# Turning the SSD rows on VectorE and through DRAM instead of on TensorE

## The chip, the cores and the metric

The kernel runs on one core of one Trainium2 chip. The metric is the device time of one launch in microseconds (us), as the median of several executions. The engines of a core each work through their own list of instructions in order and wait for each other by semaphores: TensorE (PE; its weight loads are listed as PEld), VectorE (DVE), ScalarE (ACT), GpSimd (POOL) and SyncE (SP), which here only issues transfers.

## The reference

One step of a hybrid decoder layer on T = 336 tokens (16 learned meta tokens, 256 prompt tokens, 8 sample sequences of 8 tokens), model width 2048, all in f32. Cut to its core:

```python
h = rms_norm(x, norm_w)
z, xbc, dt_raw, sc_b, sc_c, sc_h, sc_z, g_a, g_b = split_proj(h @ w_in)
# branch A: SSD. 64 heads of 64 in 8 groups, state 128, chunks of 128 tokens
xbc_c, conv_new = causal_dwconv(xbc, conv_prev, ssd_conv_w)        # width 4
xs, bm, cm = split(silu(xbc_c + ssd_conv_b))
dt = softplus(dt_raw + dt_bias); log_a = -dt * exp(a_log)
for each chunk:
    y      = (C.B^T * decay * dt) @ xs  +  exp(cumsum(log_a)) * C @ state
    state  = exp(sum(log_a)) * state + sum_j to_end_j * xs_j (x) B_j
y_a = gated_group_rms_norm(y + d_skip * xs, z, ssd_norm_w) @ w_ssd_out
# branch B: short gated conv
y_b = (sc_b * conv3(sc_c * sc_h) * silu(sc_z)) @ w_sconv_out
out = x + (sigmoid(g_a) * y_a + sigmoid(g_b) * y_b) @ w_o          # then a last rms_norm
```

Beside the two outputs, the new states of the two convolutions and of the SSD (for the prompt and for the samples) are returned.

## The kernel before

**Weights.** All weights come from HBM as blocks of 128 x 1024 f32. `wblk` (L90 to L97) takes a block through three tiles: `wraw` is loaded on SP's queue (L92), ScalarE rounds it to a high part `whi` (L94), VectorE subtracts to get the low part `wlo` (L96). Each of the three has three buffers (pool `wp`, `bufs=3`). `mm` (L109 to L115) spends a block as 24 matmuls: a first pass of 16 with `whi` (L111 against the high part of the activations, L112 against the low part) and a second pass of 8 with `wlo` (L115). There are 470 such splits in all. A projection (`proj`, `unit`) is two blocks into one PSUM tile `pj`, of which there are two.

**The group stage.** The eight groups of the SSD branch run in the pool `pb`. For a group g, `weave` traces these units of projection work one after the other: four `z_units` (two blocks each), eight `out_units` of group g-1 (one block each), for the first and last group four `gate_units`, and six `conv_units` of group g+1 (two blocks each: B, C, then the four tiles xs0 to xs3 of x). That is 28 blocks for a middle group. After each unit it advances the generator `ssd(g)`, which holds the scan of group g, by as many steps as are due (`NSTEP * past / total`), and `behind(tail)` ties each instruction of these steps behind the newest weight instruction of its engine (`latest`), so that steps stay at their place between the weight blocks. The scheduler then merges each engine's list; one list per engine is fixed when the kernel is built.

**The conv of a tile.** `conv_tile` copies the projection from PSUM to a padded tile (`pad`, two ScalarE copies, L462 and L463), applies the four taps into `cacc` (ScalarE L469, then three VectorE instructions L471) and the SiLU by a tanh (L474) and two VectorE instructions (L475, L476). The result has channels on the partitions and tokens in the free dimension.

**The scan needs rows.** The scan wants x and B with tokens on the partitions. `rows(c)`, one step for each of the chunk sets c = 0, 1, 2, does this on TensorE: four transposes of xs (L534), one of BT (L536), and beside them the product C.B (L537). VectorE multiplies by dt out of PSUM into `xdt` (L539), B is split into a high and a low part, and `cbm` takes the masked C.B. These visits, and the ones for the chunk state (L585, `state`), for y (L650) and for the samples' state (L713), stand between two weight blocks on TensorE. Later steps of the same generator are the sum over the group norm (`pr`, L701 to L705), the update of the samples' state (`up`, two halves, each two additions `h` on VectorE, L716), and the scaled y with its split (`ys` L726, `yh` L727, `yl` L728), from which group g's `out_units` in the next weave are fed.

## Time and profile before

| | |
|---|---|
| median of three runs | 1822.84 us (1822.80 to 1824.69) |
| the profiled execution | 1824.75 us, its span 1823.0 us |
| granted TensorE clock | 1.0 |
| TensorE busy | 1814.9 us, 100% of the span |
| VectorE busy | 1147.7 us, 63% |
| ScalarE busy | 828.8 us, 45% |
| GpSimd busy | 389.4 us, 21% |
| moved by DMA | 331 MB, 182 GB/s on average |
| length of a middle group's weave | 111.4 us |

In the profile, "L96 DVE TENSOR_TENSOR wlo<-wraw,whi" is an instruction of line 96 on VectorE that writes `wlo`. In a timeline the first number is the start in us from the start of the span and the second the duration; a bracket gives the idle time just before and what ended it. Matmuls overlap, so what a matmul costs TensorE is the distance from one start to the next and not the duration printed.

### The profile page before, as it was taken

How to read it: one execution, taken by the hardware profiler on the slowest of the kernel's cores; microseconds unless marked ns; L12 is line 12 of the kernel's file. 1: busy time of each engine (PE TensorE's matmuls, PEld its weight loads, DVE VectorE, ACT ScalarE, POOL GpSimd, SP SyncE). 2: the span in 40 equal slices, each digit the busy share in tenths (PEclk: the TensorE clock that was granted, in tenths of full speed). 3: DMA queues.
4: the chain of work that ended last, by engine and by line, in shares of the span. 5: the costliest groups of instructions: out<-in, count | busy, mean ns of one | idle time of the engine just before them, and what ended most of it. 6: DMA issues, size and time to landing. Idle time of an engine off the chain costs nothing.

```text
span 1823.0 us, 32410 instructions
## 1 busy us (share of the span) xinstructions
PE 1814.9 (100%) x13006; PEld 1798.0 (99%) x13006; DVE 1147.7 (63%) x1696; ACT 828.8 (45%) x1269; POOL 389.4 (21%) x398
## 2 busy tenths in 40 slices
PE   9999999999999999999999999999999999999998
PEld 9999999999999999999999999999999999999998
DVE  7745544444543335668587787877778777776544
ACT  6433333333333334645656354564546545343543
POOL 0000000000000001253162433524334252400012
PEclk9999999999999999999999999999999999999999
DMA  7444444444444446457566574665656657476553
GB/s 254 146 151 150 150 149 149 145 152 151 156 152 159 160 162 227 149 178 240 163 201 223 177 246 150 208 215 178 238 157 211 206 169 249 153 243 213 184 175 129
DMA packets 117286, 331.33 MB, mean 182 GB/s; under 512 B 20944, under 2 KB 37904, under 8 KB 117136
## 3 DMA queue, kind: packets, MB, share of 16 engines
q1 hardware_dynamic: 116272, 327.89, 55.9%
q8 instruction: 102, 1.67, 0.4%
q10 hardware_dynamic: 864, 1.38, 0.2%
q14 instruction: 48, 0.39, 0.1%
HBM read 296.34 MB, written 32.88 MB: 181 GB/s over the span
## 4 chain that ended last, share of the span: by engine, by line
PE 96%; DMA 2%; ACT 1%; DVE 1%; issue 0%; POOLq 0%; POOL 0%; SPq 0%; ACTq 0%; DVEq 0%
PE pj L111 30%; PE pj L112 30%; PE pj L115 29%; PE yb L650 2%; DMA wraw<-w 1%; PE ms L636 1%; PE pj L219 1%; PE yb L585 1%; PE pj L862 1%; ACT whi L94 0%; PE ms L534 0%; ACT W L559 0%; PE ms L219 0%; DMA ssms<-h 0%; PE yb L713 0%
## 5 line engine op out<-in xcount | busy, mean ns | idle before, releaser
L111 PE MATMUL pj<-hx,whi 128*128 128x320 f32 (+3 forms) x2880 | 864.4, 312 | 0.0
L112 PE MATMUL pj<-hx,whi 128*128 128x320 f32 (+3 forms) x2880 | 860.6, 311 | 0.0
L96 DVE TENSOR_TENSOR wlo<-wraw,whi 128x1024 fp32r<-128x1024 f32 x470 | 596.8, 1270 | 413.9 <-ACT whi L94 206.8
L94 ACT ACTIVATE whi<-wraw 128x1024 fp32r<-128x1024 f32 x470 | 496.7, 1057 | 768.0 <-PE pj L112 628.1
L111 PEld LDWEIGHTS pj<-hx,whi 128*128 128x128 f32 x2880 | 540.7, 188 | 4.6 <-ACT pad L462 1.7
L112 PEld LDWEIGHTS pj<-hx,whi 128*128 128x128 f32 x2880 | 541.5, 188 | 0.1
L115 PE MATMUL pj<-hx,wlo 128*128 128x320 f32 (+3 forms) x2880 | 485.4, 310 | 0.0
L115 PEld LDWEIGHTS pj<-hx,wlo 128*128 128x128 f32 x2880 | 440.6, 188 | 0.0
L111 PE MATMUL pj<-yh,whi 128*128 128x320 f32 x512 | 153.5, 311 | 1.2 <-ACT zs L503 0.9
L112 PE MATMUL pj<-yl,whi 128*128 128x320 f32 x512 | 152.3, 309 | 0.0
L596 POOL TENSOR_TENSOR h<-h,decS 128x512 f32<-128x512 f32 x64 | 76.4, 1227 | 147.5 <-PE ms L636 147.5
L111 PEld LDWEIGHTS pj<-yh,whi 128*128 128x128 f32 x512 | 96.2, 188 | 3.1 <-ACT zs L503 1.4
L112 PEld LDWEIGHTS pj<-yl,whi 128*128 128x128 f32 x512 | 96.3, 188 | 0.6
L115 PE MATMUL pj<-yh,wlo 128*128 128x320 f32 x512 | 95.8, 309 | 0.0
L242 POOL COPY SCS<-up 128x2 f32<-128x2 f32 x16 | 18.2, 1139 | 359.2 <-DVE up L236 329.0
L744 DVE TENSOR_TENSOR yan<-yan,pj 128x320 f32<-128x320 f32 x112 | 54.2, 485 | 62.9 <-PE pj L115 61.3
L471 DVE SCALAR_TENSOR_TENSOR cacc<-pad,V,cacc 128x360 f32<-128x360 f32 (+1 forms) x144 | 89.5, 621 | 2.0
L464 POOL COPY pad<-cs 128x24 f32<-128x24 f32 x48 | 56.2, 1172 | 126.6 <-DVE cacc L471 115.5
L115 PEld LDWEIGHTS pj<-yh,wlo 128*128 128x128 f32 x512 | 80.4, 188 | 0.0
L111 PE MATMUL pj<-vhi,whi 128*128 128x320 f32 x256 | 75.5, 308 | 0.0
L112 PE MATMUL pj<-vlo,whi 128*128 128x320 f32 x256 | 75.5, 308 | 0.0
L465 POOL COPY cs<-pad 128x3 f32<-128x3 f32 x48 | 45.0, 938 | 82.5 <-ACT pad L462 82.0
(286 smaller groups left out, 1721.7 us busy)
## 6 DMA issues: line engine op xcount, KB each, us to landing
wraw<-w SPq DMA_DIRECT2D x346, 512.0 KB, 3.9
wraw<-wso SPq DMA_DIRECT2D x64, 512.0 KB, 3.5
wraw<-wsc SPq DMA_DIRECT2D x32, 512.0 KB, 3.8
h<-h0T SPq DMA_DIRECT2D x32, 512.0 KB, 4.9
ssms<-h SPq DMA_DIRECT2D x32, 512.0 KB, 4.2
wraw<-wo SPq DMA_DIRECT2D x32, 512.0 KB, 3.9
xq_d<-xe SPq DMA_DIRECT2D x16, 320.0 KB, 3.4
W<-ac_d SPq DMA_DIRECT2D x8, 576.0 KB, 6.4
```

Source lines behind the costliest of these rows:

```text
L94: latest["act"] = nc.scalar.activation(hi[:, :n], raw[:, :n], AF.Copy).ins
L96: latest["dve"] = nc.vector.tensor_tensor(lo[:, :n], raw[:, :n], fb(hi[:, :n]), sub).ins
L111: nc.tensor.matmul(out, w, xh(k0 + k), start=first and k == 0, stop=False)
L112: nc.tensor.matmul(out, w, xl(k0 + k), start=False, stop=False)
L115: latest["pe"] = nc.tensor.matmul(out, w, xh(k0 + k), start=False, stop=last and k == nk - 1).ins
L219: nc.tensor.matmul(pu[i][:, :T - t0], w[:, o:o + P], x[:, k, t0:], start=k == 0 and j == 0, stop=k == 15 and j == 2)
L464: nc.gpsimd.tensor_copy(smp[:, :, 0:3], cs[:, 1:9, :])
L465: nc.gpsimd.tensor_copy(cs[:, 0, :], pad[:, 272:275])
L471: nc.vector.scalar_tensor_tensor(acc[:, i0:], pad[:, i0 + k:360 + k], col(V_CW, 4 * j + k), acc[:, i0:], mult, add)
L596: nc.gpsimd.tensor_tensor(split(h0[b]), split(h0[b]), bc(hv(decS[:, b, :], g), [P, 8, HP]), mult)
L650: nc.tensor.matmul(yb[q * HP:(q + 1) * HP, t, t0:t0 + n], x[:, h * HP:(h + 1) * HP], w[:, h, :], start=i == 0, stop=i == 3)
L744: nc.vector.tensor_tensor(ya[:, m, :TV], ya[:, m, :TV], pp[:, :TV], add)
```

## The change

`conv_tile` gets an argument `rows`: for B and the four tiles of x, VectorE transposes the finished tile in blocks of 32 x 32 (two instructions, 128x320 and 128x32, into the tile's own `cacc`), and four transfers of [32, 11, 32] put the blocks, now with tokens on the partitions, in their places in a DRAM tile `xr_d` of 352 x 640. These four are kept in a list and issued from ScalarE's queue by `flush()`, at the next `conv_tile` after its first tap, or in the first z unit of the next weave. `rows(c)` is gone. In its place `load(c)` reads the rows back on SP's queue, tied behind the newest weight load of SP (`latest["sp"]`, new), `cross()` computes the three C.B products in one visit, `rows_in(c)` multiplies by dt in SBUF and splits B, and `ends(c)` is the GpSimd part that stood in `weights(c)`. The steps are 25 instead of 23: `cross`, `decay(0)`, the exponential and the state loads, `decay(1)`, `weights(0)`, `weights(1)` with the loads, `rows_in(0)`, and so on. So the later steps (y, the norm's sum, the samples' state, the split of y) fall behind other units than before.

```diff
-NSTEP = 23
+NSTEP = 25
+XR = 352
...
+    xr_d = [dr.tile([XR, 640], F32, name=f"xr_d{i}") for i in range(2)]
...
     def wblk(src, n=1024):
         raw = wp.tile([P, 1024], F32, name="wraw")
-        nc.sync.dma_start(raw[:, :n], src)
+        latest["sp"] = nc.sync.dma_start(raw[:, :n], src).ins
         hi = wp.tile([P, 1024], F32R, name="whi")
         latest["act"] = nc.scalar.activation(hi[:, :n], raw[:, :n], AF.Copy).ins
         lo = wp.tile([P, 1024], F32R, name="wlo")
         latest["dve"] = nc.vector.tensor_tensor(lo[:, :n], raw[:, :n], fb(hi[:, :n]), sub).ins
         return hi, lo
+    def after(ins, a):
+        tc.add_manual_dep(ins, a.name, mybir.DependencyInfo(mybir.DependencyClass.NoSync,
+                                                            mybir.DependencyReason.DATA), reason="step")
     def behind(tail):
         for ins in reversed(nc.cur_bb.bb.instructions):
             if ins is tail:
                 break
-            for a in latest.values():
-                if ins.engine == a.engine:
-                    tc.add_manual_dep(ins, a.name, mybir.DependencyInfo(mybir.DependencyClass.NoSync,
-                                                                         mybir.DependencyReason.DATA), reason="step")
+            for k in ("act", "dve", "pe"):
+                if k in latest and ins.engine == latest[k].engine:
+                    after(ins, latest[k])
...
+        pend = []
+        def flush():
+            while pend:
+                nc.scalar.dma_start(*pend.pop(0))
+        def conv_tile(src, j, t0, out, cs, rows=None):
             pp = proj(src, t0)
...
             acc = pb.tile([P, 360], F32, name="cacc")
             nc.scalar.activation(acc[:, i0:], pad[:, i0:360], AF.Identity, bias=col(V_CB, j), scale=col(V_CW, 4 * j))
+            flush()
             for k in range(1, 4):
                 nc.vector.scalar_tensor_tensor(acc[:, i0:], pad[:, i0 + k:360 + k], col(V_CW, 4 * j + k),
...
                 acc[:, 272:360].rearrange("p (b t) -> p b t", t=11)[:, :, 3:11], add, mult)
+            if rows is not None:
+                nc.vector.transpose(acc[:, :320], out[:, :320])
+                nc.vector.transpose(acc[:, 320:XR], out[:, T - 32:])
+                to, c = rows
+                for a in range(0, P, 32):
+                    pend.append((to.rearrange("(b q) c -> q b c", q=32)[:, :, c + a:c + a + 32],
+                                 acc[a:a + 32, :XR].rearrange("p (b f) -> p b f", f=32)))
         def conv_units(g, st):
...
+            to = xr_d[g % 2]
             BT = st["BT"] = pb.tile([P, T], F32, name="BT")
-            conv_tile(w1[64 + g], 32 + g, 0, BT, cs[:, 4])
+            conv_tile(w1[64 + g], 32 + g, 0, BT, cs[:, 4], (to, 512))
             yield
...
             for t in range(4):
-                conv_tile(w1[32 + 4 * g + t], 4 * g + t, 0, xs[:, t, :], cs[:, t])
+                conv_tile(w1[32 + 4 * g + t], 4 * g + t, 0, xs[:, t, :], cs[:, t], (to, P * t))
...
                 nc.scalar.activation(th, pz, AF.Tanh, scale=0.5)
                 nc.scalar.activation(z[:, :TV], pz, AF.Copy)
+                flush()
...
+            bt = [pb.tile([P, 2, P], F32R, name="bh0", bufs=1), free[:, 1024:1280].rearrange("p (i n) -> p i n", n=P),
+                  pb.tile([P, P], F32, name="bt", bufs=1)]
+            def load(c):
+                xdt[c] = big("xdt", 3)
+                b = bt[c] if c == 2 else fb(bt[c][:, 1, :])
+                rows = xr_d[g % 2]
+                for o, r, n in ((0, P * c, P),) if c < 2 else ((0, 256, 64), (64, 336, 16)):
+                    for d, q in ((xdt[c], slice(0, 512)), (b, slice(512, 640))):
+                        after(nc.sync.dma_start(d[o:o + n], rows[r:r + n, q]).ins, latest["sp"])
+            def cross():
                 pq = ps.tile([P, 512], F32, name="ms")
-                nc.tensor.transpose(pq[:n, 0:P], BT[:, t0:t0 + n], ident)
-                nc.tensor.matmul(pq[:n, P:P + m], BT[:, t0:t0 + n], CT[:, TGT[c]:TGT[c] + m], start=True, stop=True)
-                xdt[c] = big("xdt", 3)
-                nc.vector.tensor_tensor(split(xdt[c][:n]), split(pp[:n]), bc(hv(dtt[:n, c, :], g), [n, 8, HP]), mult)
-                if c == 2:
-                    bt[c] = pb.tile([P, P], F32, name="bt", bufs=1)
-                    nc.scalar.activation(bt[c][:n], pq[:n, 0:P], AF.Copy)
-                else:
-                    bt[c] = (free[:, 1024:1280].rearrange("p (i n) -> p i n", n=P) if c else
-                             pb.tile([P, 2, P], F32R, name="bh0", bufs=1))
-                    nc.scalar.activation(bt[c][:, 0, :], pq[:, 0:P], AF.Copy)
-                    nc.vector.tensor_tensor(bt[c][:, 1, :], pq[:, 0:P], fb(bt[c][:, 0, :]), sub)
-                cbm[c] = pb.tile([P, PX], F32, name="cbm")
-                u0 = META if c == 0 else 0
-                for a, b, o in ((0, m, 0),) if c < 2 else ((META, 80, 0), (0, META, 64)):
-                    nc.vector.tensor_tensor(cbm[c][:n, o:o + b - a], pq[:n, P + a:P + b],
-                                            U[:, u0 + a:u0 + b] if c < 2 else UQ[:, a:b], mult)
+                qs = [pq[:n, o:o + m] for o, m, (_, n) in zip((0, NT[0], NT[0] + NT[1]), NT, CH)]
+                for c, (t0, n) in enumerate(CH):
+                    nc.tensor.matmul(qs[c], BT[:, t0:t0 + n], CT[:, TGT[c]:TGT[c] + NT[c]], start=True, stop=True)
+                for c, (_, n) in enumerate(CH):
+                    m = NT[c]
+                    cbm[c] = pb.tile([P, m], F32, name=f"cbm{c}", bufs=1)
+                    u0 = META if c == 0 else 0
+                    for a, b, to in ((0, m, 0),) if c < 2 else ((META, 80, 0), (0, META, 64)):
+                        nc.vector.tensor_tensor(cbm[c][:n, to:to + b - a], qs[c][:, a:b],
+                                                U[:, u0 + a:u0 + b] if c < 2 else UQ[:, a:b], mult)
+            def rows_in(c):
+                n = CH[c][1]
+                nc.vector.tensor_tensor(split(xdt[c][:n]), split(xdt[c][:n]), bc(hv(dtt[:n, c, :], g), [n, 8, HP]), mult)
+                if c < 2:
+                    b = fb(bt[c][:, 1, :])
+                    nc.scalar.activation(bt[c][:, 0, :], b, AF.Copy)
+                    nc.vector.tensor_tensor(bt[c][:, 1, :], b, fb(bt[c][:, 0, :]), sub)
...
+            def ends(c):
+                n = CH[c][1]
+                xe[c] = big("xe", 2)
+                nc.gpsimd.tensor_tensor(split(xe[c][:n]), split(xdt[c][:n]), bc(hv(tet[:n, c, :], g), [n, 8, HP]), mult)
             def weights(c):
                 n, m, w = CH[c][1], NT[c], W[c]
                 nc.vector.tensor_tensor(w[:n], w[:n], bc(cbm[c][:n, :m].unsqueeze(1), [n, 8, m]), mult)
-                xe[c] = big("xe", 2)
-                nc.gpsimd.tensor_tensor(split(xe[c][:n]), split(xdt[c][:n]), bc(hv(tet[:n, c, :], g), [n, 8, HP]), mult)
...
             yield
-            rows(0)
+            cross()
             yield
             decay(0)
             yield
             nc.scalar.activation(E, W[1], AF.Exp)
-            rows(1)
             for u in range(4):
                 h = pb.tile([P, 2, 512], F32, name="h0", bufs=4)
                 nc.sync.dma_start(h, h0T[g, :, 2 * u:2 * u + 2, :])
                 h0 += [h[:, 0, :], h[:, 1, :]]
                 h0t.append(h)
             yield
+            decay(1)
+            yield
             weights(0)
             yield
+            weights(1)
+            for c in range(3):
+                load(c)
+            yield
+            rows_in(0)
+            ends(0)
+            yield
             halve(0)
-            decay(1)
-            yield
-            rows(2)
+            rows_in(1)
             yield
             carry(0)
             state(0, pieces(0))
-            weights(1)
+            ends(1)
             yield
             halve(1)
+            rows_in(2)
             decay(2)
             yield
             carry(1)
             state(1, pieces(1))
             yield
             weights(2)
+            ends(2)
             yield
             carry(2)
             yield
```

ScalarE around the last tile of x in a middle weave. `pj_10910` and, in the second list, `pj_10983` are the PSUM tiles of xs3, which are copied to `pad1`; `whi_10998` and `whi_11077` are the high parts of the block that TensorE takes up next, the first of the next weave's z. Before:

```order
L94 ACTIVATE whi_10998<-wraw_10996 128x1024
L727 ACTIVATE yh_10896<-ys_9783 128x320
L462 ACTIVATE pad0_6709<-pj_10819 128x272
L463 ACTIVATE pad0_6709<-pj_10819 128x8x8
L727 ACTIVATE yh_10896<-ys_9783 128x320
L469 ACTIVATE cacc_10885<-pad0_6709,V_75 128x360
L94 ACTIVATE whi_11028<-wraw_11026 128x1024
L474 ACTIVATE cth_10890<-cacc_10885 128x360
L94 ACTIVATE whi_11074<-wraw_11072 128x1024
L462 ACTIVATE pad1_6710<-pj_10910 128x272
L463 ACTIVATE pad1_6710<-pj_10910 128x8x8
L469 ACTIVATE cacc_10976<-pad1_6710,V_75 128x360
L94 ACTIVATE whi_11104<-wraw_11102 128x1024
```

Changed (L94 is L96, L462 and L463 are L473 and L474, L469 is L480, L474 is L486, L727 is L767):

```order
L767 ACTIVATE yh_10969<-ys_9849 128x320 x4
L473 ACTIVATE pad1_6712<-pj_10983 128x272
L474 ACTIVATE pad1_6712<-pj_10983 128x8x8
L96 ACTIVATE whi_11077<-wraw_11075 128x1024
L480 ACTIVATE cacc_11049<-pad1_6712,V_77 128x360
L466 DMA xr_d1_76<-cacc_10952 32x11x32 x4
L96 ACTIVATE whi_11107<-wraw_11105 128x1024
L486 ACTIVATE cth_11058<-cacc_11049 128x360
L96 ACTIVATE whi_11159<-wraw_11157 128x1024
```

Before, the high parts of three blocks (`whi_10998`, `whi_11028`, `whi_11074`) stand ahead of the copies out of xs3's PSUM tile; now none does, and the first of them stands behind both copies.

VectorE at the same place, before; `wlo_11000` is the low part of that first block, `cacc_10885` belongs to xs2 and `cacc_10976` to xs3:

```order
L96 TENSOR_TENSOR wlo_11000<-wraw_10996,whi_10998 128x1024
L471 SCALAR_TENSOR_TENSOR cacc_10885<-pad0_6709,V_75,cacc_10885 128x360
L96 TENSOR_TENSOR wlo_11030<-wraw_11026,whi_11028 128x1024
L475 SCALAR_TENSOR_TENSOR xs_10640<-cth_10890,cacc_10885 128x272
L476 SCALAR_TENSOR_TENSOR xs_10640<-cth_10890,cacc_10885 128x64
L96 TENSOR_TENSOR wlo_11076<-wraw_11072,whi_11074 128x1024
L471 SCALAR_TENSOR_TENSOR cacc_10976<-pad1_6710,V_75,cacc_10976 128x360
L716 TENSOR_TENSOR h0_9966<-h0_9966,yb_10985 128x1024
L471 SCALAR_TENSOR_TENSOR cacc_10976<-pad1_6710,V_75,cacc_10976 128x360
L716 TENSOR_TENSOR h0_9968<-h0_9968,yb_10985 128x1024
L471 SCALAR_TENSOR_TENSOR cacc_10976<-pad1_6710,V_75,cacc_10976 128x360
L96 TENSOR_TENSOR wlo_11106<-wraw_11102,whi_11104 128x1024
```

Changed; `wlo_11079` is the low part of the first block, `cacc_10952` belongs to xs2 and `cacc_11049` to xs3:

```order
L768 TENSOR_TENSOR yl_10970<-ys_9849,yh_10969 128x320
L493 STREAM_TRANSPOSE cacc_10952<-xs_10682 128x320
L494 STREAM_TRANSPOSE cacc_10952<-xs_10682 128x32
L768 TENSOR_TENSOR yl_10970<-ys_9849,yh_10969 128x320 x3
L756 TENSOR_TENSOR h0_10016<-h0_10016,yb_11064 128x1024
L483 SCALAR_TENSOR_TENSOR cacc_11049<-pad1_6712,V_77,cacc_11049 128x360
L756 TENSOR_TENSOR h0_10018<-h0_10018,yb_11064 128x1024
L483 SCALAR_TENSOR_TENSOR cacc_11049<-pad1_6712,V_77,cacc_11049 128x360
L98 TENSOR_TENSOR wlo_11079<-wraw_11075,whi_11077 128x1024
L483 SCALAR_TENSOR_TENSOR cacc_11049<-pad1_6712,V_77,cacc_11049 128x360
L98 TENSOR_TENSOR wlo_11109<-wraw_11105,whi_11107 128x1024
```

Before, the low parts of three blocks stand ahead of xs3's first tap; now two taps of xs3 and the two additions `h` to the samples' state stand ahead of the first, and the transposes of xs2 and the last `yl` ahead of these.

TensorE, the first visit of the scan in a weave, before:

```order
L115 MATMUL pj_11071<-hx_80,wlo_11106 128x320 x8
L534 MATMUL ms_11137<-CR_76,xs_10640 128x128 x4
L536 MATMUL ms_11142<-CR_76,BT_10447 128x128
L537 MATMUL ms_11142<-CT_10532,BT_10447 128x112
L111 MATMUL pj_11161<-hx_80,whi_11164 128x320
L112 MATMUL pj_11161<-hx_80,whi_11164 128x320
```

Changed (L111, L112 and L115 are L116, L117 and L120):

```order
L120 MATMUL pj_11156<-hx_82,wlo_11191 128x320 x8
L566 MATMUL ms_11222<-CT_10587,BT_10425 128x112
L566 MATMUL ms_11222<-CT_10587,BT_10425 128x144
L566 MATMUL ms_11222<-CT_10587,BT_10425 80x80
L116 MATMUL pj_11242<-hx_82,whi_11245 128x320
L117 MATMUL pj_11242<-hx_82,whi_11245 128x320
```

Five transposes and one product between two weight blocks have become three products; the two other visits of the same kind are gone.

More of the change, by code (lines that the diff above doesn't have):

```diff
@@ L455, in tile_hybrid_step @@
         czs = CZ.rearrange("p (s i w) -> p s i w", s=2, w=40)
-        def conv_tile(src, j, t0, out, cs):
+        pend = []
[3 more added lines that the diff above has]
+        def conv_tile(src, j, t0, out, cs, rows=None):
             pp = proj(src, t0)
@@ L520, in ssd @@
             ys = pb.tile([P, 4, T], F32, name="ys", bufs=1)
-            W, xdt, xe, bt, cbm, hst = ([None] * 3 for _ in range(6))
+            W, xdt, xe, cbm, hst = ([None] * 3 for _ in range(5))
             W[0], W[1] = (pb.tile([P, 8, PX], F32, name="W")[:, :, :n] for n in (P - META, PX))
@@ L528, in ssd @@
             NT, TGT = (P - META, PX, 80), (META, P, 2 * P)
-            def rows(c):
-                (t0, n), m = CH[c], NT[c]
-                pp = ps.tile([P, 512], F32, name="ms")
-                for t in range(4):
-                    nc.tensor.transpose(pp[:n, t * P:t * P + P], xs[:, t, t0:t0 + n], ident)
-                pq = ps.tile([P, 512], F32, name="ms")
-                nc.tensor.transpose(pq[:n, 0:P], BT[:, t0:t0 + n], ident)
-                nc.tensor.matmul(pq[:n, P:P + m], BT[:, t0:t0 + n], CT[:, TGT[c]:TGT[c] + m], start=True, stop=True)
-                xdt[c] = big("xdt", 3)
-                nc.vector.tensor_tensor(split(xdt[c][:n]), split(pp[:n]), bc(hv(dtt[:n, c, :], g), [n, 8, HP]), mult)
-                if c == 2:
-                    bt[c] = pb.tile([P, P], F32, name="bt", bufs=1)
-                    nc.scalar.activation(bt[c][:n], pq[:n, 0:P], AF.Copy)
-                else:
-                    bt[c] = (free[:, 1024:1280].rearrange("p (i n) -> p i n", n=P) if c else
-                             pb.tile([P, 2, P], F32R, name="bh0", bufs=1))
-                    nc.scalar.activation(bt[c][:, 0, :], pq[:, 0:P], AF.Copy)
-                    nc.vector.tensor_tensor(bt[c][:, 1, :], pq[:, 0:P], fb(bt[c][:, 0, :]), sub)
-                cbm[c] = pb.tile([P, PX], F32, name="cbm")
-                u0 = META if c == 0 else 0
-                for a, b, o in ((0, m, 0),) if c < 2 else ((META, 80, 0), (0, META, 64)):
-                    nc.vector.tensor_tensor(cbm[c][:n, o:o + b - a], pq[:n, P + a:P + b],
-                                            U[:, u0 + a:u0 + b] if c < 2 else UQ[:, a:b], mult)
```

## The prediction

> **What bounds the kernel now.** I read the page first: the chain that ended last, then the costliest groups.
>
> ```profile
> PE 96%; DMA 2%; ACT 1%; DVE 1%; issue 0%; POOLq 0%; POOL 0%; SPq 0%; ACTq 0%; DVEq 0%
> L94 ACT ACTIVATE whi<-wraw 128x1024 fp32r<-128x1024 f32 x470 | 496.7, 1057 | 768.0 <-PE pj L112 628.1
> ```
>
> 96% of the chain is TensorE, so whatever leaves TensorE shortens the end, as long as TensorE never waits. Whether it waits hangs on how far the two splits run ahead. ScalarE's `whi` idles 628.1 us for L112, a matmul: it has spare time and is held by its three buffers, which TensorE must give back. To see how thin that lead gets I read the timelines of TensorE, VectorE and ScalarE around the convolution of x in a middle weave. TensorE, the starts of the `wlo` passes of three blocks (the third is xs3's last), the visit behind it and the pass of the next block, the first of z:
>
> ```profile
> 1063.02 1.40 PE L115 MATMUL pj<-hx,wlo 128*128 128x336 f32 x8
> 1066.73 1.39 PE L115 MATMUL pj<-hx,wlo 128*128 128x336 f32 x8
> 1070.44 1.39 PE L115 MATMUL pj<-hx,wlo 128*128 128x336 f32 x8
> 1071.77 0.50 PE L713 MATMUL yb<-xh,bh 32*128 32x512 f32 x4
> 1074.67 1.32 PE L115 MATMUL pj<-hx,wlo 128*128 128x320 f32 x8
> ```
>
> A block takes 3.71 us, with no gap. VectorE over the same blocks:
>
> ```profile
> 1054.52 1.22 DVE L96 TENSOR_TENSOR wlo<-wraw,whi 128x1024 fp32r<-128x1024 f32 x1
> 1055.66 0.48 DVE L704 TENSOR_TENSOR ms_a<-ms_a,ms_r 128x320 f32<-128x320 f32 x1
> 1056.06 0.44 DVE L475 SCALAR_TENSOR_TENSOR xs<-cth,cacc 128x272 f32<-128x272 f32 x1
> ...
> 1056.55 0.49 DVE L705 SCALAR_TENSOR_TENSOR ms_r<-ms_a,ms_r 128x320 f32<-128x320 f32 x1
> 1056.95 0.68 DVE L587 TENSOR_TENSOR hst<-hst,ms 128x512 f32<-128x512 f32 x1
> 1057.55 1.22 DVE L716 TENSOR_TENSOR h<-h,yb 128x1024 f32<-128x1024 f32 x1
> 1058.68 0.59 DVE L471 SCALAR_TENSOR_TENSOR cacc<-pad,V,cacc 128x360 f32<-128x360 f32 x1
> ...
> 1061.28 0.59 DVE L471 SCALAR_TENSOR_TENSOR cacc<-pad,V,cacc 128x360 f32<-128x360 f32 x1
> 1061.79 0.55 DVE L726 SCALAR_TENSOR_TENSOR ys<-ys,V,ms_r 128x320 f32<-128x320 f32 x1
> 1062.25 0.49 DVE L728 TENSOR_TENSOR yl<-ys,yh 128x320 fp32r<-128x320 f32 x1
> 1062.65 0.43 DVE L475 SCALAR_TENSOR_TENSOR xs<-cth,cacc 128x272 f32<-128x272 f32 x1
> ...
> 1064.47 1.22 DVE L96 TENSOR_TENSOR wlo<-wraw,whi 128x1024 fp32r<-128x1024 f32 x1
> ```
>
> Between two low splits VectorE has nearly 9 us of other work, without a gap. The split that ends at 1055.74 (1054.52 + 1.22) feeds the pass of 1063.02, a lead of 7.3 us; the next, ending at 1065.69, feeds the pass of 1066.73, a lead of 1.0 us. So VectorE is within 1 us of holding TensorE here.
>
> **What the change takes off TensorE.** The three old visits, from the timeline of TensorE (the one in the middle has the same forms as the first):
>
> ```profile
> 752.12 0.60 PE L534 MATMUL ms<-CR,xs 128*128 128x128 f32 x4
> 752.55 0.27 PE L536 MATMUL ms<-CR,BT 128*128 128x128 f32 x1
> 752.66 0.37 PE L537 MATMUL ms<-CT,BT 128*128 128x112 f32 x2
> 752.80 0.40 PE L111 MATMUL pj<-hx,whi 128*128 128x320 f32 x1
> 753.04 0.31 PE L112 MATMUL pj<-hx,whi 128*128 128x320 f32 x1
> 753.19 0.31 PE L111 MATMUL pj<-hx,whi 128*128 128x320 f32 x1
> ...
> 774.72 0.60 PE L534 MATMUL ms<-CR,xs 128*80 128x128 f32 x4
> 775.27 0.30 PE L537 MATMUL ms<-CT,BT 128*80 128x80 f32 x2
> ```
>
> The five transposes take 752.66 - 752.12 = 0.54 us, in the small visit 775.27 - 774.72 = 0.55: 1.63 us in a group. The three products stay. The first weight matmul behind a visit costs 0.24 us (752.80 to 753.04) where the next costs 0.15 (to 753.19); one such exit goes, 0.09. Together 1.72 us, times 8 groups **13.7 us off**.
>
> **What the change puts on the other engines.** Per tile two transposes on VectorE, priced by the nearest row, and per flush four issues on ScalarE, by the only transfers issued there:
>
> ```profile
> L643 DVE STREAM_TRANSPOSE xe<-xe 128x256 f32<-128x256 f32 x8 | 3.6, 446 | 0.3
> L181 ACTq DMA_DIRECT2D wraw<-w x2: 413/432/452, 0.7 to 1.2; - x2
> ```
>
> 446 ns for 256 columns makes 0.56 for 320 and some 0.1 for 32: 0.65 us a tile, 3.3 a group. Four issues are 1.7 us a tile; behind xs3's first tap they put the high split of the second z block to about X + 5.3 (X + 2.53, below, + 1.72 + 1.06), and it is wanted a whole block behind X, after the stop: covered. The multiplications by dt, the split of B and the GpSimd part are the same instructions with another source: nothing. At most places the lead covers the rest. Eight more loads on SP wait for the rows in DRAM, and weight loads queue behind them: xs3's rows are issued behind the first z unit's copy, its readers three units later less a three-block lead, some 11 us, so with a landing under that they cost nothing.
>
> **Where the lead goes.** With 25 steps y and all behind it come later: the norm's chain, the two additions of the first half, `ys` and `yl` now crowd before xs3's copy. On ScalarE the changed order has both copies of xs3's PSUM tile ahead of the high split of the very next block, where three splits stood ahead before. On VectorE, two additions `h` and two taps of xs3 stand ahead of its low split. So TensorE must stop there, in each of the 7 weaves that have a convolution. How long, from two sides.
>
> *From below, the chain of waits.* Let X be the moment when TensorE is through with xs3's last block. ScalarE, from the copy of xs0 and from a later split:
>
> ```profile
> 1055.98 0.40 PE L585 MATMUL ms<-xdt,b 128*128 128x512 f32 x1
> 1056.24 0.40 ACT L462 ACTIVATE pad<-pj 128x272 f32<-128x272 f32 x1 [0.22 <-PE pj L115]
> 1056.54 0.22 ACT L463 ACTIVATE pad<-pj 128x64 f32<-128x64 f32 x1
> 1056.85 0.69 ACT L469 ACTIVATE cacc<-pad,V 128x360 f32<-128x360 f32 x1
> 1063.21 1.06 ACT L94 ACTIVATE whi<-wraw 128x1024 fp32r<-128x1024 f32 x1 [0.38 <-PE pj L112]
> 1064.18 0.46 ACT L727 ACTIVATE yh<-ys 128x320 fp32r<-128x320 f32 x1
> ```
>
> The first copy starts 0.26 behind X, the second 0.30 later, then 0.31 to the next instruction, which is now `whi`; the instruction behind a split starts 0.97 behind it, so the first tap on ScalarE ends at X + 0.87 + 0.97 + 0.69 = X + 2.53. Behind it on VectorE a tap (0.51, 1061.28 to 1061.79), an `h` (1.13, 1057.55 to 1058.68), a tap and the split of 1.22: X + 5.90. TensorE would want the low part at X + 2.90 (1071.77 to 1074.67). The stop is at least **3.0 us**.
>
> *By VectorE's queue.* In the changed order, between the low split of xs2's last block and that of z's first, stand (start to start): 3 pairs of SiLU (0.49), 3 pairs of transposes (0.65), the addition to `hst` (0.60), 4 `h` (1.13), 8 taps (0.51), 7 of the norm's chain (0.40), 4 `ys` (0.46), 4 `yl` (0.40) and 3 splits (1.13, the last to its end 1.22): 1.47 + 1.95 + 0.60 + 4.52 + 4.08 + 2.80 + 1.84 + 1.60 + 3.48 = 22.3 us. TensorE needs 11.65 between the two passes (1063.02 to 1074.67), and the lead that it begins with was 7.3: 22.3 - 11.65 - 7.3 = 3.4. Into this falls the wait of the norm's chain for ScalarE:
>
> ```profile
> L701 DVE TENSOR_SCALAR ms_x<-ms 128x320 f32<-128x320 f32 x8 | 3.9, 491 | 7.8 <-ACT ms_r L700 7.8
> ```
>
> 7.8 / 8 = 1.0 us a group, giving 4.4. I take **4.0** a weave, between the queue without and with that wait. From above: VectorE is slowed at times while GpSimd works (a low split took 1.89 where 1.22 is usual), and two per group at that, with the norm's wait and ScalarE's issues in full, makes 6.
>
> ```profile
> 1030.30 1.89 DVE L96 TENSOR_TENSOR wlo<-wraw,whi 128x1024 fp32r<-128x1024 f32 x1
> ```
>
> **The sum.** 1824.75 (the profiled execution) - 13.7 + 7 x 4.0 = 1839.1. The median of the runs shown lies 1.9 below the profiled execution: **1837 us**.
>
> **The rivals**, all on the median's scale, 1822.84 - 13.7 = 1809.1 plus the stops.
>
> (a) *Only the chain of waits counts*: VectorE enters xs3 with more lead than I give it. For it: three buffers let the low split that now ends 7.3 us ahead start once the pass three blocks earlier is through, 3 x 3.71 - 1.40 = 9.7 us ahead of its own pass; less its 1.22 that is a lead of 8.5, and 4.4 shrinks to 3.2, all but the bound. Then 3.0 a weave: 1809.1 + 21 = 1830. Against it: the visits and transposes ahead of it are not fewer.
>
> (b) *The lead is lost at a second place as well.* The low split of xs3's first block, 1.0 us ahead today, gets the transposes of xs0 and xs1 ahead of it. If the norm's wait falls there, a stop there comes on top, 6 us a weave in all: 1851. Against it: that split also got rid of the `ys` and `yl`.
>
> (c) *The stop shrinks to about 2 us a weave*, because the two additions `h` run early. 1809 + 14 = 1823, no change. Against: they need the visit L713 behind xs3's last block.
>
> (d) *The cover holds, the other side: faster*, 1809. It needs the split of z's first block ahead of xs3's copies, that is an order other than the one that is fixed; against it stands the whole argument. It decides below 2 us of stop a weave.
>
> (e) *DMA becomes the bound.* Each tile goes out as 1408 runs of 128 B. The nearest rows, and the load of DMA in this stretch (the last two numbers of the window: share and GB/s):
>
> ```profile
> W<-ac_d SPq DMA_DIRECT2D x8, 448.0 KB, 5.7
> ac_d<-acx SPq DMA_DIRECT2D x1, 4.0 KB, 1.7
> 1030.00:1080.00 50.00, 50.00 (x330) 49.02 (x329) 42.47 (x67) 27.77 (x48) 21.89 (x25) 1.00 0.70 219
> ```
>
> 448 KB are 1024 runs of 448 B, 64 for each of 16 engines; (5.7 - 1.7) / 64 = 62 ns a run. A tile is 88 runs on each engine, 5.5 us, five tiles 27.5. On top of 0.70 x 50 = 35 that is 62.5 us in a stretch of 50: 12.5 too many in each of 7 weaves, 1809 + 88 = 1897. Against it: the 4 KB write is 64 runs of 64 B and lands as fast as anything, so the other bound is nothing, and the rest of the weave has room. The Trainium skill, page "DMA: Bandwidth & Descriptors", section "Specifications", asks for at least 512 B a transfer for line rate and says that below this the engine reads, modifies and writes. By that rule a run would cost two accesses, an estimate of twice the five tiles above, 35 + 55 against 50 us in 7 weaves, and the time would be 1809 + 280 = 2089; no row of this trace shows such runs in number.
>
> **How the numbers follow.** My forecast, a stop of 3.4 to 5 us, gets 0.40; (a) 0.22; (b) 0.20; (c) 0.08; (d) 0.06; (e) 0.04. The range holds the forecast with (a) and (b) and their edges: from 1827 (2.6 us a weave) to 1856 (6.7). A measurement of this kernel tells 0.2% from no change, 3.6 us; forecast, (a), (b) and (e) are beyond it, 0.86 slower, 0.08 the same, 0.06 faster.
>
> **What would show it.** In the new profile: no L534 or L536; VectorE's two transposes near 0.56 and 0.1 us; TensorE idle 1.4 us or so for `whi` and again for `wlo` at the first block behind xs3, 3 to 5 us in sum, in 7 weaves and hardly elsewhere. I am wrong if TensorE stays without gaps there, if the idle time stands at other blocks, or if waits for the weight loads or for the row loads appear.

## The result, and the profile after

The changed kernel takes 1853.24 us (median of four, 1850.16 to 1854.7) against 1823.19 us: ratio 1.0161, interval 1.0143 to 1.0179. It was forecast slower, at 1837; it lost 30 us where 14 were forecast. The profiled execution has a span of 1852.8 us, 29.8 more than before. (In the experiments below, one execution each of the runs notrans and n22 was in a much slower state and is left out, so notrans stands on a single one.) From the page of the changed kernel, the chain that ended last and two groups of TensorE with their idle time:

```profile
PE 78%; DVE 11%; DMA 6%; issue 2%; ACT 1%; POOL 1%; ACTq 0%; SPq 0%; POOLq 0%; DVEq 0%
L116 PE MATMUL pj<-hx,whi 128*128 128x320 f32 (+3 forms) x2880 | 868.5, 313 | 9.6 <-ACT whi L96 9.6
L120 PE MATMUL pj<-hx,wlo 128*128 128x320 f32 (+3 forms) x2880 | 490.1, 312 | 18.7 <-DVE wlo L98 18.7
```

TensorE's share of the chain fell from 96% to 78%: it waits, for the two splits, as forecast. All its waits come to 32.5 us of idle time as printed, 2.7 before. The longest stop but one stands behind xs3 of a middle weave; TensorE's timeline, with the wait and what ended it in brackets:

```profile
1077.72 0.51 PE L753 MATMUL yb<-xh,bh 32*128 32x512 f32 x4
1079.68 0.42 PE L116 MATMUL pj<-hx,whi 128*128 128x320 f32 x1 [1.44 <-ACT whi L96]
...
1085.68 2.47 PE L120 MATMUL pj<-hx,wlo 128*128 128x320 f32 x8 [3.40 <-DVE wlo L98]
```

The last row also shows something that was not forecast: eight matmuls in 2.47 us where they took 1.32 before (1074.67 in the prediction). The windows view of this kernel (stretch; its length; busy time of PE, PEld, DVE, ACT and POOL with counts; granted clock; DMA share; GB/s), around the first stop and around one without this effect:

```profile
850.23:853.64 3.41, 1.49 (x11) 1.22 (x9) 3.41 (x6) 1.06 (x1) 0.00 (x0) 1.00 1.04 287
853.64:857.06 3.42, 3.41 (x13) 3.41 (x14) 3.42 (x6) 1.45 (x2) 1.56 (x1) 0.50 0.96 270
857.06:860.47 3.41, 3.41 (x25) 3.41 (x25) 0.32 (x2) 1.06 (x2) 0.00 (x0) 1.00 0.96 297
...
1433.91:1437.32 3.41, 2.04 (x14) 2.04 (x15) 3.41 (x7) 2.07 (x3) 1.46 (x1) 1.00 0.98 283
1437.32:1440.73 3.41, 3.41 (x25) 3.41 (x25) 1.69 (x4) 0.40 (x2) 0.10 (x1) 1.00 0.92 328
```

TensorE was idle for 1.92 of 3.41 us (3.41 - 1.49); the granted clock of the next 3.41 us was 0.50, 13 matmuls fit where 25 fit at full clock. With 1.37 us idle (3.41 - 2.04) the clock stayed at 1.00. Seven such half-clock stretches lie in the weaves, 23.9 us, a loss of at most 12.

The idle time printed is a little less than what a stop costs, because a matmul is printed 0.31 us long while the next one starts 0.15 us later (753.04 and 753.19 in the prediction). So the ledger is counted from start to start: each distance between two starts in the traces is set against the median of the same pair of instructions where nothing waits. It gives stops +32.0 (33.8 against 1.8 before), half clock +10.3, visits saved -12.4; together +29.9 of the +29.8.

Why the stop is this long in this weave; ScalarE, then VectorE:

```profile
1078.19 0.37 ACT L473 ACTIVATE pad<-pj 128x272 f32<-128x272 f32 x1
1078.47 0.21 ACT L474 ACTIVATE pad<-pj 128x64 f32<-128x64 f32 x1
1078.57 1.05 ACT L96 ACTIVATE whi<-wraw 128x1024 fp32r<-128x1024 f32 x1
1081.54 0.69 ACT L480 ACTIVATE cacc<-pad,V 128x360 f32<-128x360 f32 x1 [1.92 <-DMA xr_d<-cacc]
1081.62 2.52 ACTq L466 DMA_DIRECT2D xr_d<-cacc  x4
```

```profile
1078.04 0.50 DVE L493 STREAM_TRANSPOSE cacc<-xs 128x320 f32<-128x320 f32 x1
1078.47 0.16 DVE L494 STREAM_TRANSPOSE cacc<-xs 128x32 f32<-128x32 f32 x1
...
1082.27 0.59 DVE L483 SCALAR_TENSOR_TENSOR cacc<-pad,V,cacc 128x360 f32<-128x360 f32 x1 [1.31 <-ACT cacc L480]
1082.78 1.21 DVE L756 TENSOR_TENSOR h<-h,yb 128x1024 f32<-128x1024 f32 x1
1083.91 0.58 DVE L483 SCALAR_TENSOR_TENSOR cacc<-pad,V,cacc 128x360 f32<-128x360 f32 x1
1084.41 1.22 DVE L98 TENSOR_TENSOR wlo<-wraw,whi 128x1024 fp32r<-128x1024 f32 x1
```

The order is the one forecast: copies, `whi`, tap; tap, `h`, tap, `wlo`. But ScalarE's tap waits 1.92 us until the rows of the tile two before it have landed in DRAM, because they lie in one of the two `cacc` buffers that it needs. That happens in two of the seven weaves (stops of 4.8 and 6.8 us as printed); in the other five the stop is 3.1 to 3.3. What ends last in those five is seen on VectorE, here in the weave before:

```profile
944.46 1.22 DVE L98 TENSOR_TENSOR wlo<-wraw,whi 128x1024 fp32r<-128x1024 f32 x1
...
964.99 0.58 DVE L483 SCALAR_TENSOR_TENSOR cacc<-pad,V,cacc 128x360 f32<-128x360 f32 x1
...
967.13 1.21 DVE L98 TENSOR_TENSOR wlo<-wraw,whi 128x1024 fp32r<-128x1024 f32 x1
```

The first row is the low part of xs2's last block, the last row that of z's first. In the 22.7 us between their ends (945.68 to 968.34) VectorE has no gap. ScalarE's tap of xs3 is through at 964.43, but VectorE takes up its own tap only at 964.99, when the work ahead of it is done. It is so in four of the five weaves, by 0.03 to 0.6 us; in the fifth VectorE waits 0.12 us for the tap. So there VectorE's queue sets the stop, with the chain of waits close behind.

### The profile page after: what moved, and what is told of

It is laid out like the page before. It is cut to its first block, busy times and chain, and to the rows that moved or that the text cites. A ratio compares the mean times of both kernels' runs of the same rounds, so it can differ in the third digit from the quotient of the medians.

```text
span 1852.8 us, 32586 instructions
## 1 busy us (share of the span) xinstructions
PE 1814.9 (98%) x12886; PEld 1795.5 (97%) x12886; DVE 1199.8 (65%) x1776; ACT 827.5 (45%) x1261; POOL 358.8 (19%) x398
## 4 chain that ended last, share of the span: by engine, by line
PE 78%; DVE 11%; DMA 6%; issue 2%; ACT 1%; POOL 1%; ACTq 0%; SPq 0%; POOLq 0%; DVEq 0%
PE pj L120 25%; PE pj L116 25%; PE pj L117 24%; DMA xr_d<-cacc 3%; DVE cacc L483 3%; DVE wlo L98 2%; DMA wraw<-w 1%; DVE h L756 1%; DMA W<-ac_d 1%; PE pj L224 1%; DMA xq_d<-xe 1%; DVE ys L693 1%; POOL zs L730 1%; PE yb L617 1%; ACT cacc L480 1%
## 5 line engine op out<-in xcount | busy, mean ns | idle before, releaser
L116 PE MATMUL pj<-hx,whi 128*128 128x320 f32 (+3 forms) x2880 | 868.5, 313 | 9.6 <-ACT whi L96 9.6
L117 PE MATMUL pj<-hx,whi 128*128 128x320 f32 (+3 forms) x2880 | 864.6, 312 | 0.0
L98 DVE TENSOR_TENSOR wlo<-wraw,whi 128x1024 fp32r<-128x1024 f32 x470 | 604.8, 1290 | 377.7 <-PE pj L120 230.6
L96 ACT ACTIVATE whi<-wraw 128x1024 fp32r<-128x1024 f32 x470 | 495.2, 1057 | 689.4 <-PE pj L117 592.1
L116 PEld LDWEIGHTS pj<-hx,whi 128*128 128x128 f32 x2880 | 544.8, 189 | 15.2 <-ACT whi L96 12.4
L117 PEld LDWEIGHTS pj<-hx,whi 128*128 128x128 f32 x2880 | 545.4, 189 | 0.1
L120 PE MATMUL pj<-hx,wlo 128*128 128x320 f32 (+3 forms) x2880 | 490.1, 312 | 18.7 <-DVE wlo L98 18.7
L120 PEld LDWEIGHTS pj<-hx,wlo 128*128 128x128 f32 x2880 | 443.5, 189 | 20.5 <-DVE wlo L98 20.5
L116 PE MATMUL pj<-yh,whi 128*128 128x320 f32 x512 | 153.0, 310 | 2.7 <-DVE yan L784 1.6
L117 PE MATMUL pj<-yl,whi 128*128 128x320 f32 x512 | 152.2, 309 | 0.0
L116 PEld LDWEIGHTS pj<-yh,whi 128*128 128x128 f32 x512 | 96.2, 188 | 5.0 <-DVE yan L784 2.4
L117 PEld LDWEIGHTS pj<-yl,whi 128*128 128x128 f32 x512 | 96.2, 188 | 0.6
L120 PE MATMUL pj<-yh,wlo 128*128 128x320 f32 x512 | 95.8, 308 | 0.0
L120 PEld LDWEIGHTS pj<-yh,wlo 128*128 128x128 f32 x512 | 80.4, 188 | 0.0
L116 PE MATMUL pj<-vhi,whi 128*128 128x320 f32 x256 | 75.5, 308 | 0.0
L117 PE MATMUL pj<-vlo,whi 128*128 128x320 f32 x256 | 75.5, 308 | 0.0
L475 POOL COPY pad<-cs 128x24 f32<-128x24 f32 x48 | 37.1, 775 | 128.9 <-DVE cacc L483 121.7
L486 ACT ACTIVATE cth<-cacc 128x360 f32<-128x360 f32 (+1 forms) x48 | 24.1, 503 | 80.4 <-DVE cacc L483 76.1
```

The costliest lines, as they stand in the source:

```text
L96: latest["act"] = nc.scalar.activation(hi[:, :n], raw[:, :n], AF.Copy).ins
L98: latest["dve"] = nc.vector.tensor_tensor(lo[:, :n], raw[:, :n], fb(hi[:, :n]), sub).ins
L116: nc.tensor.matmul(out, w, xh(k0 + k), start=first and k == 0, stop=False)
L117: nc.tensor.matmul(out, w, xl(k0 + k), start=False, stop=False)
L120: latest["pe"] = nc.tensor.matmul(out, w, xh(k0 + k), start=False, stop=last and k == nk - 1).ins
L475: nc.gpsimd.tensor_copy(smp[:, :, 0:3], cs[:, 1:9, :])
```

## The experiments

Times are medians beside runs of the kernel before on the same chip (1823 to 1824); "waits" are all of TensorE's waits in the profiled execution, as printed, "half clock" the stretches of granted clock 0.5 before the last stage.

| run | us | waits, us | half clock, us |
|---|---|---|---|
| before | 1823.2 | 2.7 | 0 |
| changed | 1853.2 | 32.5 | 23.9 |
| fill | 1844.3 | 10.7 | 0 |
| ahead | 1844.2 | 28.7 | 0 |
| n22 / n27 | 1887.3 / 1866.8 | 59.3 / 41.8 | 47.8 / 23.9 |
| steps_late | 1831.9 | 7.9 | 0 |
| notrans (one execution) | 1867.8 | 38.9 | 44.4 |
| nowrite | 1841.8 | 24.5 | 10.2 |
| neither | 1840.9 | 22.1 | 13.7 |
| noh | 1863.9 | 38.9 | 23.9 |
| own / sp / own_sp | 1857.7 / 1888.5 / 1890.2 | 37.5 / 61.2 / 60.0 | 23.9 / 44.4 / 44.4 |
| look3 / look2 | 1858.0 / 1860.4 | 35.6 / 38.8 | 34.1 / 34.1 |
| before_look3 | 1822.9 | 1.8 | 0 |
| before_add | 1839.8 | 12.2 | 6.8 |
| before_add_look3 | 1822.8 | 2.3 | 0 |
| steps_reads | 1830.4 | 8.1 | 0 |

**Is it idleness that halves the clock?** fill puts matmuls into the two waits, 7 ahead of the first z block and 12 (`idle(fill)`) between its two passes, for every group but the first (cut):

```diff
+        if fill:
+            idle(fill)
...
+            if fill and not half:
+                idle(7)
```

> The changed kernel with 19 idle matmuls (128x320, results read by nobody) in the two waits behind xs3: 7 ahead of the first z block and 12 between its two passes, 2.8 of the 3.1 us that TensorE waits in the shorter stops. Theory C (TensorE's waits of 2 to 5 us are followed by 3.41 us at half clock, and it is the idleness that does it): waits of 28 us become matmuls and a short rest, the half-clock stretches go in most weaves, 1853 - 10 = 1843. Rival (the low clock has another cause, or is only a record): clock and time as in the changed kernel, 1850 to 1855.

1844.3 us, 9 less than the changed kernel, with 19 matmuls more in each of seven weaves. TensorE's timeline there, the filler rows among the others:

```profile
847.77 1.29 PE L116 MATMUL ms<-hx,CR 128*128 128x320 f32 x7
851.47 1.92 PE L116 MATMUL ms<-hx,CR 128*128 128x320 f32 x12
853.55 1.43 PE L129 MATMUL pj<-hx,wlo 128*128 128x320 f32 x8 [0.16 <-DVE wlo L98]
```

`wlo` comes as late as before (853.55 against 853.65), but no half clock follows, in any weave: theory C holds. The 9 us come near the 10.3 counted above.

**Is it the order at xs3 alone?**

```diff
             pp = proj(src, t0)
+            if nxt is not None:               # xs3: the next weave's first z block
+                ahead.append(wblk(nxt[:, :1024]))
```

> The changed kernel, with one edit: the splits of the next weave's first z block are traced ahead of the copies of xs3's PSUM tile, so that on ScalarE and VectorE one block's splits stand ahead of xs3's conv. Theory A1 (it is the order of the lists at this one place that stops TensorE): stops under 0.5 us a weave, no half clock, 1853 - 28 - 12 = 1813, at best 1809. Rival (VectorE or ScalarE has too much to do in this stretch, whatever the order): the stop moves to the next blocks, idle time stays at 20 us or more, 1840 to 1853.

1844.2 us (ratio 1.0113, 1.0098 to 1.0128): a miss for theory A1, which asked 1813, and inside its rival's 1840 to 1853. The stops behind xs3 are short, but the waits view of this kernel has others (total, count, longest):

```profile
PE pj L117 <- ACT whi L97: 15.5, 20, 1.4
PE pj L117 <- DVE yan L788: 8.5, 7, 1.8
```

Waits fell only from 32.5 to 28.7; they are in pieces of at most 1.8 us, and the 9 us gained are about what the half clock had cost. Moving the steps instead did worse:

> The changed kernel with NSTEP = 22 instead of 25: nothing else. The steps fall behind other units, and the lists come out with at least one block's splits ahead of every copy. Theory A1 (order at one place): few stops, 1809 to 1818. Rival (too much work in the stretch): 20 us of stops or more remain, 1840 to 1853.

> The changed kernel with NSTEP = 27: y and what follows fall earlier (y right behind the last out unit, as in the kernel before), so that VectorE does ys, the norm and the first additions where it has idle time. Theory D: waits fall to 5 to 15 us, 1812 to 1825. Theory W: no better than the changed kernel, 1845 or more.

1887.3 and 1866.8 us. n22 is slower than either theory allowed, and n27 is on the side of theory W. With one block's splits ahead everywhere, n22 still stops 5.3 to 5.5 us a weave for `wlo`. A lead of one block in the lists is not a lead in time.

**The late steps alone.** steps_late keeps the changed order of steps, and turns the rows on TensorE:

> The changed kernel with its 25 steps, one C.B visit and late places, but the rows are turned by TensorE in rows_in as before: no VectorE transposes, no transfers of rows. Theory A (the late steps y, norm, h, ys, yl crowd VectorE and ScalarE before xs3, and that costs the lead): the stop behind xs3 stays, 3 us or more in 7 weaves with half-clock stretches after it, 1822.8 - 0.7 + 28 + 12 = about 1862. Theory B (the new work, transposes and row transfers, costs the lead; the late steps alone do not): no stop, 1822.

1831.9 us, neither 1862 nor 1822: the late steps cost 8 us, by waits of 7.9 us (2.7 before) in short pieces.

**Transposes, transfers, additions taken away.**

> The changed kernel without the two VectorE transposes of each tile (the transfers carry the unturned tile, so the scan's rows hold other numbers). VectorE has 5 x 0.66 = 3.3 us less to do in a weave, 2.6 of it in the stretch of xs0 to xs3. Theory D (VectorE is full in the conv stretch, and every us that it must do there beyond TensorE's time is a stop): TensorE's waits fall from 32.5 us to about 10, 1853 - 22 - 12 = 1819. Theory W (the transfers of rows do it: they hold the conv's tile and ScalarE, and load the DMA engines): waits stay above 25 us, 1840 to 1850.

> The changed kernel without the 160 transfers of rows to DRAM (the DRAM tiles are zeroed once, so x and B are zero in the scan's rows); the VectorE transposes and the reads stay. Theory D: VectorE does the same work, waits of 20 us or more stay, 1835 to 1850. Theory W: the waits go, 1810 to 1815.

> The changed kernel without the VectorE transposes and without the transfers of rows to DRAM (the DRAM tiles are zeroed once; the scan's rows are zeros); the late steps, the reads, the one C.B visit stay. Theory T (the late steps cost 8 us by the run steps_late, and the other stops come from the transposes and the transfers, each of which is enough): few stops, 1832 - 13 = 1819. Theory R (something else of the change, the reads or the rows read from SBUF, stops TensorE too): 1830 or more.

> The changed kernel with the additions to the samples' state cut to 1/16 of their columns (the samples' new state is then not complete). VectorE has about 4.1 us less in a weave, nothing of it in what the change added; half of it lies behind xs3, half behind xs1. Theory D: only the amount of VectorE's work counts, waits fall below 10 us, 1815 to 1822. Theory W: the writes still hold the tile, waits stay above 20 us, 1840 or more.

Theory D, that every us taken from VectorE comes back, fell: without the transposes it is 1867.8, beyond the range of either theory, and with less `h` 1863.9. Theory W did not hold either: without the transfers it is 1841.8 with waits of 24.5 us, which is what theory D expected of nowrite. From the waits views of notrans, TensorE and ScalarE:

```profile
PE pj L116 <- ACT whi L96: 26.9, 8, 4.5
ACT whi L96 <- DMA xr_d<-cacc: 20.2, 9, 3.9
```

Here `whi` is late, because it stands in ScalarE's list behind the transfers of rows. Without the transfers VectorE's `wlo` is late instead (13.7 us of waits). Theory T asked 1819 of neither and got 1840.9; so the added work is not all. One row of neither, of ScalarE, names a candidate: the copy of the fourth z tile stands behind a step that waits for GpSimd's product of the rows just read:

```profile
1449.71 0.63 ACT L606 ACTIVATE xw<-xe 128x512 fp32r<-128x512 f32 x1 [2.27 <-POOL xe L597]
1450.24 0.42 ACT L523 ACTIVATE cth<-pj 128x320 f32<-128x320 f32 x1
```

TensorE waited 3.27 us for that copy. No run took this apart.

**How the transfers hurt.**

> The changed kernel with a tile of its own for the turned rows, so that the conv's tile is free as soon as it is read (room for it by sharing two masked C.B tiles with a later tile). Lists around xs3 as in the changed kernel: its split behind xs3's copies. Theory H: the two long stops (4.8 and 6.8 us) fall to 3.1, waits 32.5 to about 27, two or three half-clock stretches fewer, about 1844. Theory S: the issues still stand in ScalarE's list, 1850 to 1854.

> The changed kernel with the transfers of rows issued from SP's queue and not from ScalarE's. Theory S (the transfers hurt because ScalarE's list stands behind their issue and their waits): as without transfers, 1842, with waits of 25 us for VectorE mostly. Theory H (they hurt because the conv's tile is held until they have landed, or by the load on the DMA engines): 1848 or more, ScalarE's first tap still waits for rows to land.

> Both: rows in a tile of their own, issued from SP's queue. What the transfers cost ScalarE is gone, VectorE's load is as before. Theory T: as the run without transfers, 1842. If it is clearly faster, transfers cost by other ways than ScalarE's list and the held tile were overrated; if slower than 1848, the load on SP or the DMA engines counts.

A tile of their own for the rows did not help: 1857.7, where theory H asked 1844 and theory S at most 1854. ScalarE's tap no longer waits for rows to land, but the new tile has one buffer, and now VectorE's next transpose waits for it (13.0 us in 12 waits):

```profile
964.12 0.51 DVE L494 STREAM_TRANSPOSE xrt<-xs 128x320 f32<-128x320 f32 x1 [1.80 <-DMA xr_d<-xrt]
```

So the wait for the landing moved from one engine to the other, and own doesn't tell what a tile that is really free would give. SP's queue is far worse. The waits views of sp:

```profile
SPq L466 <- DVE cacc L494: 109.0, 40, 5.7
ACT whi L96 <- DMA wraw<-w: 69.7, 34, 8.0
PE pj L116 <- ACT whi L96: 43.1, 8, 6.5
```

SP stands 109 us at the 40 first transfers of a tile, waiting for the transposes; the weight loads behind them come late, and so do `whi` and TensorE.

**Order and work apart.** Each edit so far reordered the lists as well. The next runs trace the load and both splits three (or two) blocks ahead of their matmuls, which puts two or more blocks' splits ahead of every copy out of PSUM:

```diff
             mm(pt[:, :n], hi, lo, xh, xl, 0, 8, half * 8, half == 0, half == 1)
+            refill()        # load and split block i + 3
```

> The kernel before with the same tracing three blocks ahead. Its lists have two or three blocks' splits ahead of nearly every copy already. Both theories: no change within 0.2%, 1820 to 1826; it tells how much of a gain of the run look3 belongs to the tracing ahead and not to the change.

> The changed kernel with one thing added: in the group stage the load and both splits of a weight block are traced three blocks ahead of its matmuls, so that in ScalarE's and VectorE's lists three blocks' splits stand ahead of every copy out of PSUM, in all weaves (in the changed kernel: none behind xs3, two at other places). The steps keep their places. Theory O (the order of the lists stops TensorE; the work itself fits into the weave): TensorE's waits fall below 6 us, no half clock, 1810 to 1816. Theory D (VectorE and ScalarE have too much to do in the conv stretch, whatever the order): TensorE waits for copies out of PSUM or for the scan's operands instead, 15 us or more, 1830 to 1850.

> The changed kernel with loads and splits traced two blocks ahead instead of three: two or three blocks' splits stand ahead of every copy, and z's copies stand behind fewer splits that wait for their load. If the stop of the run look3 came from copies of z standing behind splits that were not ready: stops shorter than 3 us, 1825 to 1845. Theory D (the stretch from xs0 to the fourth z block is too full for any order): 1845 to 1860.

> The kernel before (its steps, its TensorE transposes) with the new work put on top: the two VectorE transposes of each tile and the 160 transfers of rows to DRAM from ScalarE's queue; nobody reads the rows. Its lists then have one block's splits ahead of xs3's copies and of the first z block, where there were three and two. Theory A (the added work alone takes the lead away): stops behind xs3 or in the first z blocks, 15 to 30 us in all, 1838 to 1860. Theory L (only together with the late steps): 1823 to 1827.

> As the run before_add, with loads and splits traced three blocks ahead, so that the lists have three blocks' splits ahead of every copy. Without the added work this was 1822.9. Theory O (order): 1823 to 1826. Theory D (amount of work, or the transfers' waits in ScalarE's list): stops at the copies of z or conv tiles out of PSUM, 1835 or more.

> The run steps_late (late steps, TensorE transposes, 1832) with the reads of rows on SP's queue put on top, out of DRAM tiles that are zeroed once; what is read is overwritten by the rows from TensorE. Theory R (the reads, 8 a group between the weight loads, make weight loads late or crowd the DMA engines): 1840 or more, as in the run neither. If not: 1832, and what neither lost against 1819 lies elsewhere.

The clean pair is before_add and before_add_look3: the added transposes and transfers cost 16.5 us (ratio 1.0089, 1.0060 to 1.0118) in the lists as the scheduler makes them, with one stop a weave for `whi`, and nothing (0.9997, 0.9986 to 1.0008) in lists with the lead restored. In the kernel before, the work fits; what it takes away is the order. The reads cost nothing on top of the late steps (1830.4 against 1831.9).

But in the changed kernel the restored order does not help: look3 is at 1858.0, where theory O asked 1810 to 1816 and theory D at most 1850. Its waits, TensorE and SP, then SP's and ScalarE's timelines:

```profile
PE pj L127 <- ACT zs L535: 32.6, 10, 6.2
SPq L572 <- DMA xr_d<-cacc: 35.1, 9, 5.8
```

```profile
1098.31 0.33 SPq L572 DMA_DIRECT2D bh<-xr_d  x1
1104.57 0.33 SPq L572 DMA_DIRECT2D xdt<-xr_d  x1
1105.00 0.37 SPq L96 DMA_DIRECT2D wraw<-wso  x1
```

```profile
1109.64 1.06 ACT L98 ACTIVATE whi<-wraw 128x1024 fp32r<-128x1024 f32 x1 [2.90 <-DMA wraw<-wso]
...
1113.25 1.06 ACT L98 ACTIVATE whi<-wraw 128x1024 fp32r<-128x1024 f32 x1 [1.30 <-DVE W L612]
...
1114.73 0.42 ACT L534 ACTIVATE cth<-pj 128x320 f32<-128x320 f32 x1
```

SP stands at a read of rows until xs3's rows have landed (1098.6 to 1104.6); the weight load behind it is late, `whi` waits 2.90 us for it, a later `whi` another 1.30, put down to VectorE's `W`, and the copy of the fourth z tile stands behind these `whi`; TensorE waits 3.2 to 6.2 us a weave for its PSUM tile. In steps_reads there is no such wait, since nothing writes the rows in the weave. look2, with a lead of two blocks, was expected at 1825 to 1845 with stops under 3 us and came to 1860.4 with stops of 3.1 to 5.0; its SP waits 43.5 us for rows to land.

So in the changed kernel the traces show two things that stop TensorE: the lists in which the added work and the late steps have taken the splits' lead, and, once that is mended, rows that are read back before they have landed. A version with the lead restored, the steps where the kernel before had them and the reads tied further back is what these runs point to; it was not run, and whether it keeps the 12.4 us is open. Nor do these runs exclude theory D for the changed kernel, that with the late steps on top this stretch is too full for any order.

## Why the prediction was right or wrong

*What the change takes off TensorE, 13.7 us*: L534 and L536 are gone; the weight passes took the same time outside of the half-clock stretches. Counted from start to start, with the stops and the half clock left out, TensorE needs 12.4 us less (the same in look3): 1.3 less than forecast.

*Where the lead goes*: right in place, releaser and number of weaves: the first block behind xs3, `whi` then `wlo`, all seven weaves. Forecast 7 x 4.0 = 28 us; measured 28.9, reckoned as the prediction did, from the visit behind xs3 to the `wlo` pass, less the 2.90 of before (as idle time printed, 27.4: 28.3 for the two splits, less 0.9 at two blocks of xs). That the sum came out so near is in part luck. In five weaves the stop was 3.3 to 3.5, by VectorE's queue, which was counted right: 22.7 us where the prediction has 22.3, and 3.4 us of stop without the norm's wait. That wait, which made it 4.0, was not there. Rival (a), the chain of waits alone, 3.0, is only 0.6 us or less behind the queue. Two weaves were longer, 5.1 and 7.0: there the norm's wait is found (1.0 and 0.8 us), and ScalarE's tap waited for the rows' landing. The prediction did not name that second wait: the rows lie in the conv's own tile.

*The sum*: this is the step that failed. "1824.75 - 13.7 + 7 x 4.0" prices a stop at its length and what follows it at nothing. Missing is the half clock behind it, 23.9 us at 0.5, which cost 10.3 us counted from start to start; fill, which removes it, gives 9. With 10.3 the sum is 1847, against 1853.2. The smaller rest is stops at other places (3.1 us more than before), the 1.3 us of visits that were not saved and 0.9 us of stops behind xs3. The Trainium skill, page "TensorE: Matmul & The Clock Gate", Part 1, has the rule that I left out: a free-running window of 3413 ns, after an idle one half clock. The length agrees (3.41 us, and within a run all such stretches start on one 3.41 us grid); but no window here had to be idle throughout, 1.9 of 3.41 us was enough.

*Transposes and issues*: 0.50 and 0.16 us against 0.56 and 0.1; four issues between 1.5 and 2.7 us of ScalarE's queue, in the median 1.7, as forecast. That they are hidden "at most places" was right only with the order restored, in the kernel before (before_add_look3).

*Rival (b)*, a second place at xs3's first block: waits of 0.53 and 0.38 us in two weaves, for `whi` and not for the low split that (b) named. *Rivals (c) and (d)*: not seen. *Rival (e)*: wrong by a factor. The page of the changed kernel:

```profile
q10 hardware_dynamic: 59744, 8.60, 2.7%
DMA packets 182568, 345.45 MB, mean 186 GB/s; under 512 B 80848, under 2 KB 100496, under 8 KB 182416
```

ScalarE's queue went from 0.2% to 2.7% of the span for 58,880 more packets: 0.025 x 1852.8 x 16 / 58,880 = 13 ns a run, not 62. The 62 was a landing time shared out over the runs: as packets, the 448 B runs of that row took 26 ns each in the kernel before. The Trainium skill, page "DMA: Bandwidth & Descriptors", section "Specifications", says that below 512 B the engine reads, modifies and writes. The times show no sign of a second access: in the changed kernel's trace a packet of 512 B on SP's queue took 28 ns and one of 4 B 9, and the 13 of 128 B lies on the line between. (The 62 could not be doubled by that rule in any case, since the 448 B runs that it came from are below 512 B themselves.) *The reads on SP* were priced at nothing if the rows land within 11 us; they did cost nothing in the changed kernel (2.4 us of SP's waits), and it was the wait that the prediction named that stopped look3.

## What to carry to other kernels

A stop of the engine that sets the end is not priced by its length alone: when TensorE is idle for more than about half of a 3.41 us stretch, the next one runs at half clock; several short stops cost less than one long one of the same sum (28.7 us of waits without half clock in ahead). Before work is added under cover, look at how many blocks of the feeding engines' lists stand ahead of each wait, and fix that order in the program, since a scheduler may take it away; the same added work, put on the kernel before, cost 16.5 us or nothing by this alone. Data that goes through DRAM must be asked for late enough that the queue which fetches it doesn't stand still in front of the weight loads.

## What the runs showed of the hardware

Half clock follows idleness on a fixed grid of 3.41 us within a run. Over the 13 profiled executions that have such stretches, one at full clock with 1.9 us or more of idle TensorE was followed by granted clock 0.50, and one with 1.6 or less was not; between 1.64 and 1.84 both occur. Runs of 128 B from SBUF to DRAM took 13 ns each on a DMA engine, and the transfers of 352 such runs landed in 4.6 us in the median, 1.6 to 11.1. A transfer issued on a compute engine's queue took 0.31 to 1.40 us of that queue (median 0.46), and stands in its order like any instruction: what it waits for, the engine waits for (in own ScalarE's issues at 964.76 wait for the transpose of 964.12, and the `whi` behind them starts at 966.67).
